# S5 layer of a four-layer decoder trunk: state loads moved into the feed-forward layer, two pairs' states kept as two terms, weight splits tied behind the turned outputs

## The chip, the cores and the metric

The kernel runs on one core of a Trainium2 chip. The core's engines work side by side, each through its own list in order: TensorE (PE) multiplies matrices, VectorE (DVE) and ScalarE (ACT) work elementwise, GpSimd (POOL) does small things, and SyncE (SP) issues the DMA transfers. The metric is the time of one execution in microseconds (us), lower is better.

## The reference

Four layers of 1024 channels on 256 positions, each a mixer, a normed residual, a dense SwiGLU feed-forward layer, and a second normed residual; the mixers are HGRN2, mLSTM, S5, HGRN2. All is fp32. The change is in the S5 mixer: 64 groups of 16 channels, each with 64 complex states that decay by a diagonal factor.

```python
u = x @ w_in
dt = exp(log_dt)[:, None];  abar = exp((a_re + 1j * a_im) * dt)
bbar = (abar - 1) / a * b
h[t] = abar * h[t-1] + bbar @ u[t]          # per group, causal
y[t] = re(c @ h[t]) + d_skip * u[t]
za, zb = split(gelu(y) @ w_out)
out = za * sigmoid(zb)
```

## The kernel before

A weight of 1024 x 256 words (1 MB) is loaded by `fetch` on SP's queue into one of three staging buffers; `stage_next` later makes two pairs from it, a high part on ACT (`hi`, L149) and the low rest on DVE (`lo`, L150). A product is three matmuls, high by high, high by low, low by high (L180 to L182). Since the three buffers go round, a load can start only when the low split of the weight three places ahead is done. A scheduler sets the order on each engine; the code adds edges where it wants another. `self.behind` holds one instruction, and `order` puts each low split behind it.

The S5 mixer (`s5`) works with time in 4 chunks of 64 positions. `project` gives u; `land` turns it on DVE into `s5u` (L1161). The 64 groups go in four pairs p = 0 to 3 of two blocks (e). For a pair:

- `load_in` brings two matrices `bm` (512 KB each) and the table of rotations `cs` (768 KB); `load_out` brings `ch` (512 KB) and two `cw` (256 KB each).
- `inputs` (PE, L1184, 128 small matmuls) gives the states' inputs `g`; a pair's `s5u` must be there.
- `forth` (DVE): four products L1195 and L1196 rotate the inputs, L1197 adds, four scans L1200 run along time with decay `rr`.
- `back` (DVE): products L1206 and L1207 rotate back into the scratch tiles `s5rot`, and the add L1209 writes the states `s5hs`, one of two buffers by turns.
- `outputs` (PE): 32 matmuls of `s5u` with `cw` (L1223) and 64 of the states with `ch` (L1230) into two banks of tag `t`, then gelu on ACT into `ys`.
- `turn`: four transposes of `ys` on PE (L1240), the high cast on ACT (L93, `xx`) and the low rest on DVE (L1245, `xx`). The turn frees the bank it read, and its result is what the next output matmuls read.

Between them `few` issues some of the output product's matmuls (`a`, weights `w_so`) to fill PE. The order in the code is: turn 0 in the middle of the last piece of u, turn 1 before pair 3's inputs, turn 2 before pair 3's outputs, turn 3 last. Each `back` sets `self.behind`.

Of the kernel before, what the change touches and what calls it, by code (L numbers as in the profile page):

```python
# [2 lines left out]

# [6 lines left out]
F32 = mybir.dt.float32  # L10
# [4 lines left out]
ALU = mybir.AluOpType  # L15
AX = mybir.AxisListType

P = 128
# [10 lines left out]
MASKED = (1, 2, 4, 8, 16)  # L29
BIG = 1e30  # L30
AHEAD = 1
ROWS = (0, 1, NBLK - 1)


class Trunk:
    def __init__(self, ctx, tc, aps):
        self.ctx, self.tc, self.nc, self.a = ctx, tc, tc.nc, aps
        mk = lambda name, bufs, **kw: ctx.enter_context(tc.tile_pool(name=name, bufs=bufs, **kw))
        self.const = mk("const", 1)
        self.stage = mk("stage", 3)  # L40
        self.split = mk("split", 8)
        self.xp = mk("xp", 3)
        self.gbp = mk("gbp", 1)
        self.small = mk("small", 4)
        self.ps = mk("ps", 2, space=bass.MemoryType.PSUM)
        self.dram = mk("dram", 1, space=bass.MemoryType.DRAM)
        self.n = 0
        c = self.const
        self.ident = c.tile([P, P], F32, name="ident")
        self.root = c.tile([P, 8], F32, name="root")  # L50
        self.nc.gpsimd.memset(self.root, -0.5)
        self.eps = c.tile([P, 1], F32, name="eps")
        self.nc.gpsimd.memset(self.eps, LN_EPS)
        self.xx = c.tile([P, KD, 2, S], F32R, name="xx")
        self.xh, self.xl = (self.xx[:, :, i] for i in range(2))
        self.x = [None, None]
        self.lb = None
        self.tabled, self.loaded, self.table_name = [], None, None
        self.plan, self.ready, self.staged, self.taken = [], {}, 0, 0
        self.fetched, self.landed = 0, {}  # L60
        self.behind = None

    def uid(self, s):
        self.n += 1
# [73 lines left out]

    def order(self, i, j):

        if j is not None:
            dep = mybir.DependencyInfo(mybir.DependencyClass.NoSync, mybir.DependencyReason.DATA)
            self.tc.add_manual_dep(i, j.name, dep, reason="order")

# [745 lines left out]
    def s5_prepare(self):  # L890


        nc, a = self.nc, self.a
# [4 lines left out]
        c = self.s5const  # L898
# [18 lines left out]
        def temps(*shape):  # L917
            n = int(np.prod(shape))
            dims = "abcd"[: len(shape)]
            out = []  # L920
            for tag, bufs in (("t0", 1), ("t1", 1)):
                t = tile_(tag, [P, 1024], bufs=bufs)[:, :n]
                kw = dict(zip(dims, shape))
                out.append(t.rearrange(f"p ({' '.join(dims)}) -> p {' '.join(dims)}", **kw))
            return out
# [84 lines left out]

        def table_out(b):
            cs, neg = k["cs"], temps(16, 64)[0]
            nc.scalar.mul(neg, cs[:, 1], -1.0)
            for i in range(2):
                for row, x in enumerate((cs[:, 0], neg, cs[:, 1])):
                    nc.sync.dma_start(self.s5_cs[2 * b + i][:, :, row].rearrange("p e (f c) -> p e f c", f=4),
                                      x[:, 8 * i : 8 * i + 8].rearrange("p (e f) c -> p e f c", e=2))
# [92 lines left out]
    def s5(self, gb):  # L1110
# [14 lines left out]
            for i in range(2):  # L1125
                out_piece(n, h, k0, i)

        with tc.tile_pool(name=self.uid("s5"), bufs=1, reuse_waits="tile") as mp, \
                tc.tile_pool(name=self.uid("sw"), bufs=2, reuse_waits="tile") as wp:
            tl = lambda tag, shape, bufs=2: wp.tile(shape, F32, tag=tag, name=self.uid(tag), bufs=bufs)  # L1130
            u = mp.tile([P, 32, 64], F32, name="s5u")
            rr = [mp.tile([P, 2, 4, 64], F32, name=f"s5rr{i}") for i in range(2)]
            hs = [mp.tile([P, 2, 2, 4, 65], F32, name=f"s5hs{i}") for i in range(2)]
            rot = [mp.tile([P, 2, 2, 256], F32, name=f"s5rot{i}") for i in range(3)]
            for r in rr:
                nc.gpsimd.memset(r[:, :, :, 0:1], 0.0)
            for h in hs:
                nc.gpsimd.memset(h[:, :, :, :, 0:1], 0.0)
            bm, cw, ch, tables, wi, pxs = {}, {}, {}, {}, {}, {}

            def load(dst, tag, src, i, bufs=2):
# [10 lines left out]
                for b in (2 * p, 2 * p + 1):  # L1152
                    load(cw, "cw", self.s5_cw, b, 4)

            load_in(0)
            load_out(0)

            def land(ps, f0, h):

# [41 lines left out]

            def back(p):

                x, g, y = rot
                h, cs = hs[p % 2], tables[p]
                tt(x, g, cs[:, :, 0:1].broadcast_to([P, 2, 2, 256]), ALU.mult)  # L1206
                tt(y, g[:, :, ::-1], cs[:, :, 2:0:-1], ALU.mult)  # L1207
                many = lambda t: t.rearrange("p e r (f c) -> p (e r f) c", f=4)
                return tt(h.rearrange("p e r f c -> p (e r f) c")[:, :, 1:], many(x), many(y), ALU.add).ins  # L1209

            pieces, todo = [], []
            col = lambda f: slice(f * P, (f + 1) * P)
# [1 line left out]
            def outputs(p):  # L1214


                py, h = [self.bank("t") for _ in range(2)], hs[p % 2]
                at = lambda g, e, f: py[g][64 * e : 64 * e + 64, 64 * f : 64 * f + 64].rearrange("p (j c) -> p j c", j=4)
                for f in range(4):
                    for g in range(2):  # L1220
                        for e in range(2):
                            w = cw[2 * p + e].rearrange("p (f j g c) -> p f j g c", f=4, j=4, g=2)
                            nc.tensor.matmul(at(g, e, f), u[:, 8 * p + 4 * e + f, :], w[:, f, :, g, :], start=f == 0, stop=False, skip_group_check=True)  # L1223
                for f in range(4):
                    for i in range(2):
                        for g in range(2):
                            for e in range(2):
                                r = slice(64 * g, 64 * g + 64)
                                c = ch[p].rearrange("p i j (f c) -> p i j f c", f=8)
                                nc.tensor.matmul(at(g, e, f), h[r, e, i, f, 0:64], c[r, i, :, 4 * e + f, :], start=False, stop=f == 3 and i == 1, skip_group_check=True)  # L1230
                ys = tl("ys", [P, 4, P], 1)
                for g in range(2):
                    self.act(ys.rearrange("p j (f g c) -> p g f j c", f=4, g=2)[:, g], py[g][:, 0:256].rearrange("p (f j c) -> p f j c", f=4, j=4), AF.Gelu_apprx_tanh)
                todo.append((ys, 2 * p))

            def turn(ys, k):

                pt = self.bank("t")
                for j in range(4):
                    nc.tensor.transpose(pt[:, col(j)], ys[:, j], self.ident)  # L1240
                k = slice(k, k + 2)
                oh, ol = (x[:, k].rearrange("p e (c j) -> p j e c", j=4) for x in (self.xh, self.xl))
                src = pt.rearrange("p (j e c) -> p j e c", j=4, e=2)
                self.act(oh, src, AF.Copy)
                tt(ol, src, oh.bitcast(F32), ALU.subtract)  # L1245
                pieces.extend((h, k.start, i) for i in range(2) for h in range(2))

            def few(n):
# [4 lines left out]
            land(project_part(1, 0, "g"), 0, 1)  # L1253
            self.table("gelu_apprx_tanh_and_others")
            inputs(0)
            load_in(1)
            self.fetch()
            last = project_part(1, 1, "a")
            forth(0)
            land(last, 8, 1)  # L1260
            more = project(1, 0, "a")
            self.behind = back(0)
            load_out(1)
            self.fetch()
            inputs(1)
            load_in(2)
# [4 lines left out]
            land(more, 16, 0)  # L1271
            more = project(1, 1, "a", lambda: turn(*todo.pop(0)))
            land(more, 16, 1)
            self.behind = back(1)
            load_out(2)
            inputs(2)
            load_in(3)
# [4 lines left out]
            few(3)  # L1282
            turn(*todo.pop(0))
            few(1)
            self.behind = back(2)
            load_out(3)
            inputs(3)
            outputs(2)
# [4 lines left out]
            few(3)  # L1293
            turn(*todo.pop(0))
            few(1)
            self.behind = back(3)
            few(2)
            outputs(3)
            self.stage_next()
            few(2)  # L1300
            self.stage_next()

            self.behind = None
            first = banks[0]
            banks[0] = [self.bank("g") for _ in range(2)]
            out_part(1, 0, 0)
# [1 line left out]
            out_part(1, 0, 2)  # L1308
            second, banks[0] = banks[0], first
            turn(*todo.pop(0))  # L1310
        with tc.tile_pool(name=self.uid("so"), bufs=2, reuse_waits="tile") as op:
            self.table("sigmoid_and_others")
            outs = [[], []]

            def gated(h):
                pa, pb = banks[h]
                sg = op.tile([P, 512], F32, tag="sg", name=self.uid("sg"))
                ho = op.tile([P, 512], F32, tag="ho", name=self.uid("ho"), bufs=4)
                self.act(sg, pb, AF.Sigmoid)
                tt(ho, sg, pa, ALU.mult)  # L1320
                outs[h].append(ho)

            gb = gb()
            for h in range(2):
                out_part(0, h, 6)
                gated(h)
            banks = [second, [self.bank("a") for _ in range(2)]]
            for h in range(2):
                for k in (4, 6) if h == 0 else range(0, KD, 2):
                    out_part(1, h, k)  # L1330
                gated(h)
                self.layernorm(h, outs[h], gb)
# [158 lines left out]
```

## Time and profile before

| what | value |
|---|---|
| median of 3 runs | 1262.62 us (1261.2 to 1262.99) |
| the profiled execution | 1260.97 us, span 1259.2 us, mean granted clock 0.997 |
| PE, DVE, ACT busy | 1240.1, 957.9, 705.8 us |
| share of the chain that ended last | PE 94%, DVE 3% |
| the S5 layer's four pairs | about 653 to 717 us of the span |

The span is the stretch from the first to the last instruction of one profiled execution. Busy shares are averages over stages; the chain is followed back from the last instruction, at each step to what released it. A wait is named by the waiting line and by what ended last of what it waited for. The granted clock is 1.0 at full speed of PE.

### The profile page before, as it was taken

The numbers are of one execution on the slowest core, as the hardware profiler recorded it, in microseconds if no ns is written. First come the engines' busy times: TensorE is split into PE (matmuls) and PEld (weight loads), VectorE is DVE, ScalarE is ACT, GpSimd is POOL, SyncE is SP. The second block draws the span as 40 slices with busy tenths as digits, with TensorE's granted clock in tenths as the row PEclk, the third lists the DMA queues.
The fourth block names the chain that finished last, engine by engine and source line by source line (L and its number), as shares of the span: only waits on it lengthen the run. The fifth ranks groups of instructions, "written<-read, shape, count | busy, mean of one in ns | idle before, by whom it ended". The sixth has DMA issues, their size and how long they took to land.

```text
span 1259.2 us, 21464 instructions
## 1 busy us (share of the span) xinstructions
PE 1240.1 (98%) x8525; PEld 1037.3 (82%) x8525; DVE 957.9 (76%) x1704; ACT 705.8 (56%) x1146; POOL 35.9 (3%) x58
## 2 busy tenths in 40 slices
PE   9999999999999999999997999999999999999997
PEld 7977788888788888888886788888889878888886
DVE  6887899876787799866599787666586887766664
ACT  7755576565467555666443456555459654555551
POOL 0000000000100100000000000000000000000000
PEclk9999999999999999999999999999999999999999
DMA  8733466765273276656577446454545432755530
GB/s 324 287 136 134 170 220 230 251 229 200 101 294 134 101 259 233 236 202 231 177 301 290 181 171 247 184 201 181 187 158 220 166 135 99 269 178 190 192 142 34
DMA packets 46340, 247.91 MB, mean 197 GB/s; under 512 B 5504, under 2 KB 11024, under 8 KB 19872
## 3 DMA queue, kind: packets, MB, share of 16 engines
q1 hardware_dynamic: 46112, 246.46, 53.8%
q8 instruction: 67, 1.10, 0.3%
q14 instruction: 33, 0.27, 0.1%
q0 software_dynamic: 128, 0.09, 0.0%
HBM read 233.94 MB, written 12.58 MB: 196 GB/s over the span
## 4 chain that ended last, share of the span: by engine, by line
PE 94%; DVE 3%; DMA 1%; ACT 1%; issue 0%; SPq 0%; DVEq 0%; ACTq 0%
PE g L210 19%; PE g L180 10%; PE g L182 10%; PE g L181 10%; PE g L213 10%; PE a L181 9%; PE a L180 9%; PE a L182 9%; PE a L369 1%; PE t L271 1%; PE a L663 1%; PE t L1074 1%; PE a L543 1%; DVE s5rot L1200 1%; DMA w<-in_w_hg 1%; DMA first<-in_first 1%
## 5 line engine op out<-in xcount | busy, mean ns | idle before, releaser
L150 DVE TENSOR_TENSOR lo<-w,hi 128x1024 fp32r<-128x1024 f32 x388 | 470.7, 1220 | 117.2 <-ACT hi L149 109.7
L149 ACT CAST hi<-w 128x1024 fp32r<-128x1024 f32 x388 | 405.5, 1051 | 195.8 <-PE a L181 109.9
L210 PE MATMUL g<-xx,hi 128*128 128x512 f32 x1024 | 358.2, 395 | 0.0
L213 PE MATMUL g<-xx,lo 128*128 128x256 f32 x1024 | 267.1, 281 | 0.0
L210 PEld LDWEIGHTS g<-xx,hi 128*128 128x128 f32 x1024 | 186.7, 188 | 34.6
L213 PEld LDWEIGHTS g<-xx,lo 128*128 128x128 f32 x1024 | 192.5, 188 | 10.3
L180 PE MATMUL g<-hi,xx 128*128 128x512 f32 (+1 forms) x416 | 167.2, 403 | 2.3 <-ACT xx L290 1.8
L182 PE MATMUL g<-lo,xx 128*128 128x512 f32 (+1 forms) x416 | 165.1, 399 | 0.1
L181 PE MATMUL g<-hi,xx 128*128 128x512 f32 (+1 forms) x416 | 164.7, 397 | 0.0
L350 ACT COPY sum<-g 128x256 f32<-128x256 f32 x128 | 47.7, 373 | 147.8 <-PE g L210 147.6
L180 PE MATMUL a<-hi,hh 128*128 128x512 f32 x328 | 129.4, 395 | 0.0
L182 PE MATMUL a<-lo,hh 128*128 128x512 f32 x328 | 129.3, 394 | 0.0
L181 PE MATMUL a<-hi,hl 128*128 128x512 f32 x328 | 128.8, 393 | 0.0
L351 DVE TENSOR_TENSOR sum<-g,sum 128x256 f32<-128x256 f32 x128 | 54.1, 423 | 69.4 <-ACT sum L350 68.8
L180 PEld LDWEIGHTS g<-hi,xx 128*128 128x128 f32 x416 | 78.3, 188 | 20.1 <-ACT xx L290 2.7
L182 PEld LDWEIGHTS g<-lo,xx 128*128 128x128 f32 x416 | 78.2, 188 | 18.2 <-DVE lo L150 1.4
L181 PEld LDWEIGHTS g<-hi,xx 128*128 128x128 f32 x416 | 78.3, 188 | 15.9
L182 PEld LDWEIGHTS a<-lo,hh 128*128 128x128 f32 x328 | 61.5, 188 | 14.5
L181 PEld LDWEIGHTS a<-hi,hl 128*128 128x128 f32 x328 | 61.5, 188 | 14.3 <-DVE hl L340 0.2
L180 PEld LDWEIGHTS a<-hi,hh 128*128 128x128 f32 x328 | 61.5, 188 | 12.5 <-ACT hh L339 0.2
L180 PE MATMUL g<-xx,hi 128*128 128x256 f32 x192 | 54.5, 284 | 0.2 <-DVE k L614 0.2
L182 PE MATMUL g<-xx,hi 128*128 128x256 f32 x192 | 54.3, 283 | 0.0
(305 smaller groups left out, 1754.9 us busy)
## 6 DMA issues: line engine op xcount, KB each, us to landing
w<-in_w_gu SPq DMA_DIRECT2D x88, 1024.0 KB, 4.9
w<-in_w_dn SPq DMA_DIRECT2D x44, 1024.0 KB, 4.8
w<-in_w_hg SPq DMA_DIRECT2D x30, 1024.0 KB, 5.2
w<-in_w_ml SPq DMA_DIRECT2D x12, 1024.0 KB, 4.9
gb<-in_ln SPq DMA_DIRECT2D x8, 1024.0 KB, 4.8
w<-in_w_ho SPq DMA_DIRECT2D x8, 1024.0 KB, 4.8
w<-in_w_so SPq DMA_DIRECT2D x8, 1024.0 KB, 6.7
s5b<-st SPq DMA_DIRECT2D x16, 256.0 KB, 2.0
```

Source lines behind the costliest of these rows:

```text
L149: self.nc.scalar.copy(hi, x)
L150: i = self.nc.vector.tensor_tensor(lo, x, hi.bitcast(F32), ALU.subtract).ins
L180: mm(ps, lh, rh, start=start, stop=False)
L181: mm(ps, ll, rh, start=False, stop=False)
L182: mm(ps, lh, rl, start=False, stop=stop)
L210: whole = lambda: mm(ps, hi[:, c], self.xx[:, k].rearrange("p i t -> p (i t)"), start=k == 0, stop=k == KD - 1)
L213: mm(ps[:, S:], lo[:, c], self.xh[:, k], start=False, stop=False)
L271: nc.tensor.transpose(pt[:, (k % 4) * P : (k % 4 + 1) * P], z[:, k * P : (k + 1) * P], self.ident)
L350: nc.scalar.copy(t, ps[:, S:])
L351: nc.vector.tensor_tensor(t, ps[:, 0:S], t, ALU.add)
L369: nc.tensor.matmul(down[h][n], hidden(h, j, b)[x], dn[j][b][y][:, f], start=False, stop=(x, y, b) == steps[-1])
L543: nc.tensor.matmul(o, att[:, 2 * h + hd % 2, :], v[:, h, c], start=True, stop=h == 0)
```

## The change

- The loads of all `bm` and `cs` of pairs 0 and 1 (four times 512 KB, twice 768 KB) are asked for at the layer's start. The state buffers now lie in three pools (`sh`, `sm`, `sw`), and those of `bm` and `cs` are free early enough that on SP's queue the six loads stand in feed-forward layer 1, between its weights; `ch` and `cw` of these pairs stay behind the first output weight. The second output weight and the parameters `gb` now stand ahead of pair 2's `bm`, the third ahead of pair 3's first `bm` and pair 2's `cs`.
- The states `s5hs` are flat tiles of 1025 words; column 63 of each table is set to zero on GpSimd when the tables are built, so that a run of 64 words starts with a zero or with the state before.
- For pairs 1 and 2 (`TWO`) the back products write `s5hs0` and `s5hs1` themselves, there is no add, and `outputs` runs 128 state matmuls, both terms summed in the bank.
- `self.behind` holds two instructions, the end of the last `back` and the last turn's low rest, and each low split is put behind both.

Lines move by two at the start and by up to ten at the end (L1184 is L1190, L1195/L1196 L1201/L1202, L1197 L1203, L1200 L1206, L1206/L1207 L1216/L1217, L1209 L1219, L1223 L1234, L1230 L1240, L1240 L1250, L1245 L1255, L149/L150 L151/L152, L93 L95).

```diff
+TWO = (1, 2)
...
-        self.behind = None
+        self.behind = {}
...
-        if j is not None:
+        for j in j.values():
...
             cs, neg = k["cs"], temps(16, 64)[0]
+            nc.gpsimd.memset(cs[:, :, :, 63:64], 0.0)
...
+            hp, mp, wp = (pools.enter_context(tc.tile_pool(name=self.uid(n), bufs=1, reuse_waits="tile")) for n in ("sh", "sm", "sw"))
+            tl = lambda tag, shape, bufs=2: (wp if tag in ("bm", "cs") else hp).tile(shape, F32, tag=tag, name=self.uid(tag), bufs=bufs)
...
-            hs = [mp.tile([P, 2, 2, 4, 65], F32, name=f"s5hs{i}") for i in range(2)]
+            hs = [hp.tile([P, 1025], F32, name=f"s5hs{i}") for i in range(2)]
...
-            load_in(0)
-            load_out(0)
+            for p in range(2):
+                load_in(p)
+                load_out(p)
...
             def back(p):
...
-                h, cs = hs[p % 2], tables[p]
+                cs, flat = tables[p], lambda t: t.rearrange("p e r x -> p (e r x)")
+                at = lambda h: h[:, 1:].rearrange("p (e r x) -> p e r x", e=2, r=2)
+                x, y = map(at, hs) if p in TWO else (x, y)
                 tt(x, g, cs[:, :, 0:1].broadcast_to([P, 2, 2, 256]), ALU.mult)
-                tt(y, g[:, :, ::-1], cs[:, :, 2:0:-1], ALU.mult)
...
+                i = tt(y, g[:, :, ::-1], cs[:, :, 2:0:-1], ALU.mult)
+                if p not in TWO:
+                    i = tt(hs[p % 2][:, 1:], flat(x), flat(y), ALU.add)
+                self.behind["back"] = i.ins
...
+                py, terms = [self.bank("t") for _ in range(2)], hs if p in TWO else hs[p % 2 :][:1]
...
+                for f, i, h in itertools.product(range(4), range(2), terms):
+                    for g, e in itertools.product(range(2), range(2)):
+                        r, x = slice(64 * g, 64 * g + 64), 64 * (8 * e + 4 * i + f)
+                        last = f == 3 and i == 1 and h is terms[-1]
+                        nc.tensor.matmul(at(g, e, f), h[r, x : x + 64], c[r, i, :, 4 * e + f, :], start=False, stop=last, skip_group_check=True)
...
-                tt(ol, src, oh.bitcast(F32), ALU.subtract)
+                self.behind["turn"] = tt(ol, src, oh.bitcast(F32), ALU.subtract).ins
...
-            self.behind = None
...
             turn(*todo.pop(0))
+            self.behind = {}
```

What it does to the order shows at three places. The first is ACT, from the gelu of pair 1's outputs to turn 2's cast. `hi` are the high casts of the output weights; `xx` are the turns' casts. Before:

```order
L93 ACTIVATE ys1295_7462<-t1293_7412 128x4x4x16 [waits PE_49,Activation_49]
L93 ACTIVATE ys1295_7462<-t1294_7413 128x4x4x16 [waits PE_49]
L149 CAST hi1316_7662<-w1300_7483 128x1024
L93 ACTIVATE xx_83<-t1305_7507 128x4x2x64 [waits PE_49]
L149 CAST hi1324_7769<-w1318_7666 128x1024 [waits DMAHW4_49]
L149 CAST hi1326_7773<-w1318_7666 128x1024
L93 ACTIVATE ys1313_7645<-t1311_7595 128x4x4x16 [waits PE_49,Activation_49]
L93 ACTIVATE ys1313_7645<-t1312_7596 128x4x4x16 [waits PE_49]
L149 CAST hi1328_7789<-w1319_7668 128x1024 [waits DMAHW5_49]
L149 CAST hi1330_7793<-w1319_7668 128x1024
L93 ACTIVATE xx_83<-t1320_7688 128x4x2x64 [waits PE_49]
```

And after:

```order
L95 ACTIVATE ys1296_7498<-t1294_7416 128x4x4x16 [waits PE_49,Activation_49]
L95 ACTIVATE ys1296_7498<-t1295_7417 128x4x4x16 [waits PE_49]
L151 CAST hi1329_7856<-w1320_7735 128x1024 [waits DMAHW5_49,PE_49]
L95 ACTIVATE xx_83<-t1306_7543 128x4x2x64 [waits PE_49]
L151 CAST hi1331_7860<-w1320_7735 128x1024 [waits PE_49]
L95 ACTIVATE ys1314_7712<-t1312_7630 128x4x4x16 [waits PE_49,Activation_49]
L95 ACTIVATE ys1314_7712<-t1313_7631 128x4x4x16 [waits PE_49]
L151 CAST hi1336_7880<-w1335_7878 128x1024 [waits DMAHW7_49,DVE_49,PE_49]
L95 ACTIVATE xx_83<-t1321_7755 128x4x2x64 [waits PE_49]
```

The first high cast of the fifth output weight (`w1320`, which was `w1319`) moves ahead of turn 1's cast, and that of the sixth (`w1335`, which was `w1334`) ahead of turn 2's. The second place is DVE, from pair 2's scans to pair 3's first products. Before:

```order
L1200 SCALAR_TENSOR_TENSOR s5rot1_6907<-s5rr0_6902,s5rot0_6906 128x256 x3
L1245 TENSOR_TENSOR xx_83<-t1305_7507,xx_83 128x4x2x64 [waits Activation_49]
L1206 TENSOR_TENSOR s5rot0_6906<-s5rot1_6907,cs1274_7222 128x1024 [waits DVE_49]
L1207 TENSOR_TENSOR s5rot2_6908<-s5rot1_6907,cs1274_7222 128x1024
L1209 TENSOR_TENSOR s5hs0_6904<-s5rot0_6906,s5rot2_6908 128x16x64 [waits DVE_49]
L150 TENSOR_TENSOR lo1315_7659<-w1300_7483,hi1314_7658 128x1024 [waits DMAHW7_49]
```

And after:

```order
L1206 SCALAR_TENSOR_TENSOR s5rot1_6912<-s5rr0_6907,s5rot0_6911 128x256 x3
L1216 TENSOR_TENSOR s5hs0_6909<-s5rot1_6912,cs1275_7227 128x1024 [waits DVE_49,PE_49]
L1217 TENSOR_TENSOR s5hs1_6910<-s5rot1_6912,cs1275_7227 128x1024 [waits PE_49]
L1255 TENSOR_TENSOR xx_83<-t1306_7543,xx_83 128x4x2x64 [waits Activation_49]
L152 TENSOR_TENSOR lo1316_7726<-w1301_7519,hi1315_7725 128x1024 [waits DMAHW2_49]
```

The add is gone, and turn 1's low rest moves from ahead of the back products to behind them. Turns 0 and 2 move likewise: turn 0's from ahead of pair 1's scans to behind them, turn 2's from between pair 3's back products to behind its state add. The third place is PE, from turn 2's transposes on. `a` is the output product, `t` the outputs of pair 3. Before, the first of the 32 matmuls with `cw` stand ahead of the wait for turn 2's low rest:

```order
L180 MATMUL a1301_7485<-hi1314_7658,xx_83 128x512 [waits Activation_49]
L180 MATMUL a1303_7487<-hi1314_7658,xx_83 128x512
L1223 MATMUL t1321_7716<-cw1307_7525,s5u_6901 64x64 [waits DMAHW2_49,PE_49]
L1223 MATMUL t1321_7716<-cw1308_7527,s5u_6901 64x64 [waits DMAHW3_49]
...
L181 MATMUL a1301_7485<-hi1314_7658,xx_83 128x512 [waits DVE_49]
L182 MATMUL a1301_7485<-lo1315_7659,xx_83 128x512
```

After, all 32 stand behind the output product's matmuls:

```order
L182 MATMUL a1302_7521<-hi1315_7725,xx_83 128x512 [waits Activation_49]
L183 MATMUL a1302_7521<-hi1315_7725,xx_83 128x512 [waits DVE_49]
L184 MATMUL a1302_7521<-lo1316_7726,xx_83 128x512
...
L184 MATMUL a1304_7523<-lo1316_7726,xx_83 128x512
L1234 MATMUL t1322_7783<-cw1308_7560,s5u_6906 64x64 [waits DMAHW2_49,PE_49]
L1234 MATMUL t1322_7783<-cw1309_7562,s5u_6906 64x64 [waits DMAHW3_49]
```

PE waits for the low rest right behind the first matmul of that group, with 11 of them, the 32 and pair 3's state matmuls still to come. In pair 2's outputs likewise: from the third matmul of L1234 on, all of them and the 128 state matmuls stand behind turn 1's low rest, whose bank they use.

More of the change, by code (lines that the diff above doesn't have):

```diff
@@ L1 @@
+import itertools
 import math
@@ L1126, in out_part @@
                 out_piece(n, h, k0, i)
-        with tc.tile_pool(name=self.uid("s5"), bufs=1, reuse_waits="tile") as mp, \
-                tc.tile_pool(name=self.uid("sw"), bufs=2, reuse_waits="tile") as wp:
-            tl = lambda tag, shape, bufs=2: wp.tile(shape, F32, tag=tag, name=self.uid(tag), bufs=bufs)
+        with ExitStack() as pools:
+            hp, mp, wp = (pools.enter_context(tc.tile_pool(name=self.uid(n), bufs=1, reuse_waits="tile")) for n in ("sh", "sm", "sw"))
+            tl = lambda tag, shape, bufs=2: (wp if tag in ("bm", "cs") else hp).tile(shape, F32, tag=tag, name=self.uid(tag), bufs=bufs)
             u = mp.tile([P, 32, 64], F32, name="s5u")
-            rr = [mp.tile([P, 2, 4, 64], F32, name=f"s5rr{i}") for i in range(2)]
-            hs = [mp.tile([P, 2, 2, 4, 65], F32, name=f"s5hs{i}") for i in range(2)]
+            rr = [hp.tile([P, 2, 4, 64], F32, name=f"s5rr{i}") for i in range(2)]
+            hs = [hp.tile([P, 1025], F32, name=f"s5hs{i}") for i in range(2)]
             rot = [mp.tile([P, 2, 2, 256], F32, name=f"s5rot{i}") for i in range(3)]
@@ L1137, in s5 @@
             for h in hs:
-                nc.gpsimd.memset(h[:, :, :, :, 0:1], 0.0)
+                nc.gpsimd.memset(h[:, 0:1], 0.0)
             bm, cw, ch, tables, wi, pxs = {}, {}, {}, {}, {}, {}
@@ L1204, in back @@
                 x, g, y = rot
-                h, cs = hs[p % 2], tables[p]
+                cs, flat = tables[p], lambda t: t.rearrange("p e r x -> p (e r x)")
+                at = lambda h: h[:, 1:].rearrange("p (e r x) -> p e r x", e=2, r=2)
+                x, y = map(at, hs) if p in TWO else (x, y)
                 tt(x, g, cs[:, :, 0:1].broadcast_to([P, 2, 2, 256]), ALU.mult)
-                tt(y, g[:, :, ::-1], cs[:, :, 2:0:-1], ALU.mult)
-                many = lambda t: t.rearrange("p e r (f c) -> p (e r f) c", f=4)
-                return tt(h.rearrange("p e r f c -> p (e r f) c")[:, :, 1:], many(x), many(y), ALU.add).ins
+                i = tt(y, g[:, :, ::-1], cs[:, :, 2:0:-1], ALU.mult)
+                if p not in TWO:
+                    i = tt(hs[p % 2][:, 1:], flat(x), flat(y), ALU.add)
+                self.behind["back"] = i.ins
             pieces, todo = [], []
@@ L1214, in outputs @@
             def outputs(p):
-                py, h = [self.bank("t") for _ in range(2)], hs[p % 2]
+                py, terms = [self.bank("t") for _ in range(2)], hs if p in TWO else hs[p % 2 :][:1]
                 at = lambda g, e, f: py[g][64 * e : 64 * e + 64, 64 * f : 64 * f + 64].rearrange("p (j c) -> p j c", j=4)
@@ L1223, in outputs @@
                             nc.tensor.matmul(at(g, e, f), u[:, 8 * p + 4 * e + f, :], w[:, f, :, g, :], start=f == 0, stop=False, skip_group_check=True)
[L1224 to L1230, printed above, removed]
+                c = ch[p].rearrange("p i j (f c) -> p i j f c", f=8)
+                for f, i, h in itertools.product(range(4), range(2), terms):
[3 more added lines that the diff above has]
+                        nc.tensor.matmul(at(g, e, f), h[r, x : x + 64], c[r, i, :, 4 * e + f, :], start=False, stop=last, skip_group_check=True)
                 ys = tl("ys", [P, 4, P], 1)
@@ L1261, in s5 @@
             more = project(1, 0, "a")
-            self.behind = back(0)
-            load_out(1)
+            back(0)
             self.fetch()
@@ L1273, in s5 @@
             land(more, 16, 1)
-            self.behind = back(1)
+            back(1)
             load_out(2)
@@ L1284, in s5 @@
             few(1)
-            self.behind = back(2)
+            back(2)
             load_out(3)
@@ L1295, in s5 @@
             few(1)
-            self.behind = back(3)
+            back(3)
             few(2)
```

1 line of the change is left out of this document (removed).

## Prediction

> **What bounds the kernel now.** I read the page's busy table and its chain first, then the busy time by stage, then what TensorE waits for, and last the timelines of the S5 layer.
>
> ```profile
> PE 1240.1 (98%) x8525; PEld 1037.3 (82%) x8525; DVE 957.9 (76%) x1704; ACT 705.8 (56%) x1146; POOL 35.9 (3%) x58
> PE 94%; DVE 3%; DMA 1%; ACT 1%; issue 0%; SPq 0%; DVEq 0%; ACTq 0%
> ```
>
> TensorE (PE) is busy 98% of 1259.2 us and carries 94% of the chain that ends last; VectorE (DVE) carries 3%. The change can only gain where the chain leaves PE. That is one stretch, the four pairs of the S5 layer. In the table by stage (stretch, its length, busy time of PE, PEld, DVE, ACT, POOL, granted clock, DMA share, GB/s):
>
> ```profile
> 480.00:490.00 10.00, 10.00 (x56) 8.60 (x56) 9.92 (x20) 5.84 (x12) 0.00 (x0) 1.00 0.51 200
> 644.00:648.00 4.00, 3.54 (x19) 2.73 (x18) 3.85 (x11) 0.37 (x1) 0.72 (x1) 1.00 1.03 424
> 671.00:680.00 9.00, 6.99 (x185) 5.52 (x187) 8.50 (x11) 2.30 (x3) 0.00 (x0) 1.00 0.86 302
> 680.00:693.00 13.00, 10.21 (x276) 8.44 (x278) 12.93 (x16) 5.11 (x7) 0.00 (x0) 1.00 0.93 360
> 690.60:694.00 3.40, 1.43 (x66) 1.32 (x66) 3.37 (x4) 2.00 (x3) 0.00 (x0) 1.00 0.86 354
> 694.00:697.40 3.40, 3.40 (x10) 2.63 (x9) 3.40 (x6) 2.36 (x4) 0.00 (x0) 0.51 0.04 14
> ```
>
> From 671 to 693 us DVE is full and PE is idle for 2.0 + 2.8 us. After the idle stretch at 690.6 the granted clock is 0.51 for 3.4 us. PE's waits in the whole layer:
>
> ```profile
> PE t L1230 <- DVE s5hs L1209: 2.5, 1, 2.5
> PE g L1184 <- issue: 1.9, 1, 1.9
> PE g L1184 <- DVE s5u L1161: 1.6, 1, 1.6
> PE a L181 <- DVE xx L1245: 0.5, 1, 0.5
> ```
>
> The state add L1209 and the low half of a turn, L1245, are what PE waits for. The second wait has no releaser; in the chain it comes at the end of a burst of small matmuls, and DVE works through it, so it costs nothing later. The chain (start, us, what) there and at the end of pair 3:
>
> ```profile
> 661.00 1.92 PE g L1184 x126
> 662.92 1.87 issue
> 665.09 1.08 PE t L1223 x32
> 703.13 0.50 PE a L181
> 705.73 0.61 PE t L1223 x16
> 706.34 1.09 PE t L1230 x64
> ```
>
> At 703.13 PE is released by the turn's L1245, and at 707.43 (706.34 + 1.09) pair 3's outputs are done; from there PE has enough work, so what 707.43 becomes is what the time gains or loses. DVE's timeline (start, us, line; idle in brackets) gives the steps that lead there:
>
> ```profile
> 670.45 1.22 DVE L1197 TENSOR_TENSOR s5rot<-s5rot,s5rot 128x1024 f32<-128x1024 f32 x1
> 672.10 1.07 DVE L1245 TENSOR_TENSOR xx<-t,xx 128x512 fp32r<-128x512 f32 x1 [0.43 <-ACT xx L93]
> 673.08 2.43 DVE L1200 TENSOR_TENSOR_SCAN s5rot<-s5rr,s5rot 128x256 f32<-128x256 f32 x4
> 675.54 1.23 DVE L1206 TENSOR_TENSOR s5rot<-s5rot,cs 128x1024 f32<-128x1024 f32 x1
> 676.68 0.71 DVE L1161 STREAM_TRANSPOSE s5u<-a 128x512 f32<-128x512 f32 x1
> 677.32 1.18 DVE L1207 TENSOR_TENSOR s5rot<-s5rot,cs 128x1024 f32<-128x1024 f32 x1
> 678.53 1.23 DVE L1209 TENSOR_TENSOR s5hs<-s5rot,s5rot 128x1024 f32<-128x1024 f32 x1
> 679.67 1.22 DVE L150 TENSOR_TENSOR lo<-w,hi 128x1024 fp32r<-128x1024 f32 x1
> 680.81 0.68 DVE L1195 TENSOR_TENSOR s5rot<-g,cs 128x512 f32<-128x512 f32 x1
> 683.21 1.22 DVE L150 TENSOR_TENSOR lo<-w,hi 128x1024 fp32r<-128x1024 f32 x1
> 684.34 1.22 DVE L1197 TENSOR_TENSOR s5rot<-s5rot,s5rot 128x1024 f32<-128x1024 f32 x1
> 685.59 2.44 DVE L1200 TENSOR_TENSOR_SCAN s5rot<-s5rr,s5rot 128x256 f32<-128x256 f32 x4
> 692.43 1.22 DVE L150 TENSOR_TENSOR lo<-w,hi 128x1024 fp32r<-128x1024 f32 x1
> 695.96 1.21 DVE L150 TENSOR_TENSOR lo<-w,hi 128x1024 fp32r<-128x1024 f32 x1
> 701.96 1.11 DVE L1245 TENSOR_TENSOR xx<-t,xx 128x512 fp32r<-128x512 f32 x1
> 704.22 1.23 DVE L1209 TENSOR_TENSOR s5hs<-s5rot,s5rot 128x1024 f32<-128x1024 f32 x1
> ```
>
> From start to start a 128x1024 operation takes 1.14 us (1.25 where the next needs its result), the scan 2.46, s5u 0.64, the back product L1207 1.21, four products 2.40 (680.81 to 683.21), a turn's low half 0.98. ScalarE (ACT) and the queue on SyncE (SP) give the price of a weight:
>
> ```profile
> 447.97 2.00 ACT L149 CAST hi<-w 128x1024 fp32r<-128x1024 f32 x2 [2.98 <-DMA w<-in_w_gu]
> 679.37 1.05 ACT L149 CAST hi<-w 128x1024 fp32r<-128x1024 f32 x1 [3.22 <-DMA w<-in_w_so]
> 684.94 1.10 ACT L93 ACTIVATE xx<-t 128x512 fp32r<-128x512 f32 x1 [2.24 <-PE t L1240]
> 697.24 0.33 SPq L108 DMA_DIRECT2D w<-in_w_so  x1
> 701.99 2.00 ACT L149 CAST hi<-w 128x1024 fp32r<-128x1024 f32 x2 [0.75 <-DMA w<-in_w_so]
> ```
>
> The load at 697.24 goes out as the low split at 695.96 ends (697.17), because the two share a buffer, and its cast starts at 701.99: 4.75 us from issue to cast.
>
> **The change, part by part.**
>
> *Loads in the feed-forward layer.* Of the S5 loads four bm and two cs (3.5 MB), leave the stretch at 640 us. What it is worth there: at 644 to 648 the DMA share is 1.03, but PE's only idle there, 0.46 us, is not put to a load; I take 0, with 0.46 as the gain's bound. In feed-forward layer 1 they add 3.5 MB at some 420 GB/s (the rate of that saturated row), 8.3 us of transfer, where a stage such as 480 to 490 has a DMA share of 0.51 and PE fully busy. Of the casts between 440 and 540 us one waits for a load, the 2.98 us at 447.97, and PE does not stop for it. The worst place is a bm pair, 1 MB, right ahead of a weight: 2.4 us later. I take 0, bounds 0 and +2.4. The two memsets on GpSimd (POOL busy 3%) and the flat states cost nothing: the operations keep their sizes.
>
> *Two terms.* Pairs 1 and 2 lose L1209, 1.14 us of DVE each, and PE gets 64 more state matmuls for each, 1.09 us by the row at 706.34. Both lie where PE has idle time, so they cost PE nothing while it waits for DVE.
>
> *The ties.* DVE, walked in its new order from the end of L1197 at 671.67 (up to there its order is as before): scan to 674.15; the turn's low half, now behind the scan, to 675.15 (its 0.43 us of waiting is gone); back product to 676.3, s5u to 676.9, back product to 678.1; no add; low split to 679.25 where before it ended at 680.81; products to 681.65, low split to 682.8. So far 1.54 us are won: 1.14 for the add, 0.40 for the wait. Then add 684.05, scan 686.5, back products 687.65 and 688.85.
>
> Next comes turn 1's low half, and this is where I see the gain go. On ACT the high cast of the fifth output weight now stands ahead of turn 1's own cast (the first order list of the section on the change). That weight's load goes out when the low split frees its buffer, at 682.8; its cast starts 4.75 us later, 687.55, ends 688.6; the turn's cast ends 689.7, and the low half on DVE 690.7. PE waits for it before pair 2's outputs. In its timeline before, the inputs of pair 3 were
>
> ```profile
> 686.23 1.99 PE L1184 MATMUL g<-s5u,bm 128*32 128x64 f32 x128
> ```
>
> and ended at 688.2. Now they end about there too: s5u is ready 0.4 us sooner (676.9 for 677.3), pair 1's state matmuls last 1.1 us longer, and their wait for L1209 is gone (0.4, with hs0 written first). So PE idles from 688.3 to 690.7, 2.4 us; behind the wait are 30 of L1234 and the 128 state matmuls. Before, DVE began the next low split at 692.43; now at 690.7, 1.7 us ahead instead of 2.5.
>
> From 690.7: low split 691.85, products 694.25, low split 695.4, add 696.65, scan 699.1, back products 700.25 and 701.45, state add 702.6. Behind it, no longer between the back products, stands turn 2's low half. Its cast again has a weight's cast ahead of it: load out at 695.45, cast 700.2 to 701.25, turn's cast to 702.35. So DVE is the later one: 702.6 to 703.65, where L1245 before ended at 703.07 (701.96 + 1.11). What DVE won, 2.8 us at the state add (before 705.45), is spent by standing 2.3 us further back.
>
> PE then has 11 matmuls (703.13 to 705.73, 2.60), all 32 of L1234 (1.08; before 16 were done ahead) and the 64 state matmuls (1.09): 703.7 + 4.77 = 708.5, against 707.43. **+1.05 us**.
>
> *What hides in the waits.* The burst on PE is now 128 + 120 matmuls in pair 1 and 30 + 128 in pair 2. The row at 662.92 shows a stop of 1.87 us in such a burst. In pair 1 it would delay turn 1's transposes, whose cast began at 684.94 before and cannot begin before 688.6 now, 3.7 us of room; in pair 2 PE ends its outputs at 693.95, plus 24 matmuls of 0.236 us (2.60 / 11) and four transposes some 700, plus 1.87 still ahead of 702.35. So 0, bounds 0 and +1.9.
> [...]
>
> *Clock.* By the rows at 690.6 and 694.0, 1.43 us of work in 3.4 us was followed by 3.4 us at 0.51. Before, that loss of some 1.7 us lay in PE's spare time ahead of 703. Now the first wait (2.4 us) can bring it on again and it is absorbed as before, since PE is early at the second wait. If it is not brought on there, PE reaches the second wait at 700 and idles for up to 3.4 us but for one matmul, and the half clock falls on the closing 4.77 us: up to +1.7. I take 0 and keep +1.7.
> [...]
>
> The sum against the profiled execution (1260.97 us; span 1259.2): 1262.0. That execution is 1.65 us under the median of the runs, 1262.62; put on the median: 1263.7.
>
> **The rivals.** *The half clock falls on the end* (+1.7 more, +2.7): 1265.4. For it: a gap of the same length did it once, and the second wait now stands straight ahead of pair 3's outputs. Against: the first wait is likely to use it up. It decides if PE works less than about 1.4 of the 3.4 us ahead of 703.7.
> *The saved DVE time arrives, faster.* If turn casts on ACT are not held by the weights, turn 1's low half starts at 688.85 and all that follows moves up by 0.85: only +0.2. For a real gain PE must get to pair 3's outputs without the turn: then the state add at 702.6, 2.8 us earlier than before, would set the end, 1262.62 - 2.8 = 1259.8. The outer bound is all waits, 6.5, less the added 2.2 us of matmuls: -4.3, 1258.3. Against: PE's order puts the 11 matmuls that read turn 2's low half ahead of pair 3's outputs.
> *Weights late in feed-forward layer 1*, +2.4 alone, +3.4 with the sum: 1266.1. Against: full PE and a DMA share of 0.5 to 0.8 there. It decides if a moved load stands ahead of a weight whose cast has under 2.4 us to spare.
> *The change does nothing that lasts*: 1262.6, from the same balance with both terms 0.5 us smaller.
>
> **How the numbers follow.** About 0.2% (2.5 us) is what a measurement of this kernel can tell from no change: under 1260.1 is faster, above 1265.1 slower. The forecast with its near kin (0 to +2): 0.58. Half clock at the end 0.2, late weights 0.07: of their 0.27 nearly all is slower. The saved time arrives: 0.15, nearly all faster. Range 1259.8 (the state add sets the end) to 1266.2 (either of the slower two).
>
> **What would show it.** In the changed profile: PE waits for L1255 of turn 1 near 688 to 691 in place of L1209's 2.5 us; ACT's cast of w_so with a DMA wait right ahead of the turn's cast, twice; DVE reaches pair 3's state add near 701.5, then L1255; pair 3's state matmuls end near 708.5; no new PE wait between 440 and 640. Wrong if L1255 of turn 2 ends before 702 (faster) or the granted clock between 703 and 709 is near 0.75 (slower).

## The result: 0.35% slower, and where the time went

| | before | after |
|---|---|---|
| median | 1262.17 us | 1266.06 us |
| runs | 1260.98 to 1262.99 | 1265.38 to 1268.86 |
| profiled execution, span | 1260.97, 1259.2 us | 1265.98, 1264.2 us |

The ratio is 1.0035, with a 95% interval of 1.0024 to 1.0045: 3.9 us slower by the medians, 5.0 by the profiled executions. The forecast was no measurable change, 1263.7.

The page of the changed kernel, busy table and chain:

```profile
PE 1245.4 (99%) x8653; PEld 1041.9 (82%) x8653; DVE 955.3 (76%) x1702; ACT 706.1 (56%) x1146; POOL 36.5 (3%) x60
PE 95%; DVE 2%; ACT 1%; issue 1%; DMA 1%; SPq 0%; DVEq 0%; ACTq 0%
```

DVE lost two records and 2.6 us, PE gained 128, and "issue", time in which an engine waits for nothing the profile shows, has come into the chain with 1%. By stage, as before (length, busy time of PE, PEld, DVE, ACT, POOL, clock, DMA share, GB/s):

```profile
440.00:500.00 60.00, 60.00 (x297) 49.67 (x296) 57.28 (x119) 33.44 (x52) 1.53 (x5) 1.00 0.81 297
671.00:680.00 9.00, 9.00 (x193) 7.06 (x191) 8.93 (x12) 5.43 (x6) 0.00 (x0) 1.00 0.79 279
680.00:693.00 13.00, 10.09 (x147) 8.38 (x145) 8.74 (x11) 2.61 (x4) 0.00 (x0) 0.74 0.49 181
693.00:703.00 10.00, 9.45 (x306) 8.05 (x306) 9.71 (x13) 1.90 (x4) 0.00 (x0) 1.00 0.28 98
```

The moved loads raise the DMA share of feed-forward layer 1, from 0.65 between 440 and 500 us in the kernel before to 0.81, and PE stays full there (60.00 of 60 us in both). From 671 to 680 us PE's idle time is gone. The loss begins between 680 and 693: PE idles 2.9 us, the granted clock is 0.74, and DVE, full before, is busy for 8.74 of 13 us. What PE waits for:

```profile
PE t L1240 <- issue: 3.5, 2, 2.9
PE g L1190 <- issue: 2.2, 1, 2.2
PE a L183 <- DVE xx L1255: 0.8, 1, 0.8
PE a L182 <- ACT xx L95: 0.6, 1, 0.6
```

The 2.5 us for the state add and the 1.6 us for s5u are gone, as the change has it. In their place stands a stop of 2.9 us in pair 1's state matmuls (L1240) with no releaser. The chain shows what hangs on it:

```profile
680.09 1.43 PE t L1240 x84
681.52 2.91 issue
684.43 1.33 PE t L1240 x27
...
691.62 0.45 PE t L1250 x4
692.09 1.10 ACT xx L95
...
706.30 1.08 DVE xx L1255
707.42 0.50 PE a L183
...
710.25 1.08 PE t L1234 x32
711.33 1.09 PE t L1240 x64
```

After 84 of the last 120 state matmuls PE stands still until 684.43. The 36 that are left (the chain shows 27 of them) take 1.33 us where 84 had taken 1.43, and the long matmuls behind them start 0.43 us apart until 690.3, not 0.23. It is half clock for 6.8 us, by the row

```profile
683.70:690.50 6.80, 6.07 (x47) 4.94 (x47) 5.04 (x7) 1.65 (x3) 0.00 (x0) 0.50 0.64 236
```

So the last of turn 1's transposes end at 692.1, and DVE waits for turn 1's cast. DVE's timeline:

```profile
678.07 1.21 DVE L152 TENSOR_TENSOR lo<-w,hi 128x1024 fp32r<-128x1024 f32 x1
687.66 1.22 DVE L1217 TENSOR_TENSOR s5hs<-s5rot,cs 128x1024 f32<-128x1024 f32 x1
693.22 1.19 DVE L1255 TENSOR_TENSOR xx<-t,xx 128x512 fp32r<-128x512 f32 x1 [4.34 <-ACT xx L95]
705.16 1.23 DVE L1219 TENSOR_TENSOR s5hs<-s5rot,s5rot 128x1024 f32<-128x1024 f32 x1
706.30 1.06 DVE L1255 TENSOR_TENSOR xx<-t,xx 128x512 fp32r<-128x512 f32 x1
```

and ACT's:

```profile
689.51 1.04 ACT L151 CAST hi<-w 128x1024 fp32r<-128x1024 f32 x1 [3.15 <-PE a L183]
692.09 1.09 ACT L95 ACTIVATE xx<-t 128x512 fp32r<-128x512 f32 x1 [1.54 <-PE t L1250]
704.02 1.05 ACT L151 CAST hi<-w 128x1024 fp32r<-128x1024 f32 x1 [3.93 <-DMA w<-in_w_so]
```

Pair 3's outputs end at 712.42 (711.33 + 1.09) where they ended at 707.43: 5.0 us, which is the whole difference of the spans.

### The profile page after: what moved, and what is told of

Read it like the earlier page. It is cut to its first block, busy times and chain, and to the rows that moved or that the text cites. A ratio compares the mean times of both kernels' runs of the same rounds, so it can differ in the third digit from the quotient of the medians.

```text
span 1264.2 us, 21732 instructions
## 1 busy us (share of the span) xinstructions
PE 1245.4 (99%) x8653; PEld 1041.9 (82%) x8653; DVE 955.3 (76%) x1702; ACT 706.1 (56%) x1146; POOL 36.5 (3%) x60
## 3 DMA queue, kind: packets, MB, share of 16 engines
q8 instruction: 68, 1.11, 0.3%
## 4 chain that ended last, share of the span: by engine, by line
PE 95%; DVE 2%; ACT 1%; issue 1%; DMA 1%; SPq 0%; DVEq 0%; ACTq 0%
PE g L212 19%; PE g L182 10%; PE g L184 10%; PE g L183 10%; PE g L215 10%; PE a L182 9%; PE a L183 9%; PE a L184 9%; PE a L371 1%; PE t L273 1%; PE a L665 1%; PE t L1077 1%; PE a L545 1%; DMA first<-in_first 1%; PE g L1190 0%
## 5 line engine op out<-in xcount | busy, mean ns | idle before, releaser
L152 DVE TENSOR_TENSOR lo<-w,hi 128x1024 fp32r<-128x1024 f32 x388 | 470.4, 1220 | 117.3 <-ACT hi L151 109.9
L151 ACT CAST hi<-w 128x1024 fp32r<-128x1024 f32 x388 | 405.6, 1051 | 197.1 <-PE a L183 115.0
L183 PE MATMUL g<-hi,xx 128*128 128x512 f32 (+1 forms) x416 | 164.8, 397 | 0.0
L183 PE MATMUL a<-hi,hl 128*128 128x512 f32 x328 | 128.8, 393 | 0.0
L183 PEld LDWEIGHTS g<-hi,xx 128*128 128x128 f32 x416 | 78.3, 188 | 15.9
L183 PEld LDWEIGHTS a<-hi,hl 128*128 128x128 f32 x328 | 61.5, 188 | 14.3 <-DVE hl L342 0.2
```

The lines of the kernel that those rows point to most:

```text
L151: self.nc.scalar.copy(hi, x)
L152: i = self.nc.vector.tensor_tensor(lo, x, hi.bitcast(F32), ALU.subtract).ins
L183: mm(ps, ll, rh, start=False, stop=False)
```

## The experiments

Theory A: the stop is PE running out of instructions. The page of the changed kernel shows a queue of instructions:

```profile
q8 instruction: 68, 1.11, 0.3%
```

That is 68 packets of 16 KB (1.11 MB / 68) beside 2 x 8653 PE records (a weight load and a matmul each), one for about 255 records, that is 127 matmuls; the page of before has 67 beside 2 x 8525, about 255 again. By this count they are blocks of PE's instructions. At 84 in 1.43 us, 127 state matmuls last about 2.2 us. Counted in the trace, the stops in the S5 layer come after matmul record 4411 before, and after 4411, 4792 and 5047 in the changed kernel: 3 x 127 and 2 x 127.5 apart. After the edge at record 4665 was passed, at 679.2, an instruction packet started at 682.15 and ended at 683.1, and PE went on at 684.43: 5.2 us after the edge, when the 127 records behind it were through in 2.3. Rivals: B, the moved loads; C, the tie behind the turns; D, the places of the turns' low halves and casts alone, as in the prediction, only dearer.

**No pair in two terms.**

```diff
-TWO = (1, 2)
+TWO = ()
```

> The changed kernel with no pair in two terms: adds back, 64 state matmuls for each pair; the moved loads and the tie stay. Theory A (the burst of 128 input and 120 state matmuls runs PE out of instructions for 2.9 us, the half clock follows, and turn 1's cast comes 2.4 us late): the stop in pair 1's outputs is gone, no wait put to 'issue' there above 0.5 us, turn 1's cast near 685; turns 1 and 2 stand where they stood before the change, so 1261 to 1263. Theory B (the moved loads cost it): 1265 to 1267. Theory C (the tie costs it): 1265 to 1267, DVE idle ahead of a turn.

Measured: 1262.03 us, ratio to the kernel before 1.0 (0.9991 to 1.0009). PE's waits, and ACT's turn 1:

```profile
PE t L1240 <- DVE s5hs L1219: 2.5, 1, 2.5
684.75 1.10 ACT L95 ACTIVATE xx<-t 128x512 fp32r<-128x512 f32 x1 [2.92 <-PE t L1250]
```

The stop in pair 1's outputs is gone, and the old wait for the state add is back. Moved loads and tie cost nothing without the two terms: B and C fall as causes by themselves.

**No tie behind the turn.**

```diff
-                self.behind["turn"] = tt(ol, src, oh.bitcast(F32), ALU.subtract).ins
+                tt(ol, src, oh.bitcast(F32), ALU.subtract)
```

> The changed kernel with the low splits tied behind the back products alone, as before the change, two terms and moved loads kept. In the order turn 1's low half then stands behind both low splits, further back still. Theory A: the stop of about 2.9 us stays, and the time is no better: 1265.5 to 1269. Theory C (the tie costs it): 1262 to 1263.5. Theory B: 1266.

Measured: 1266.93 us, 1.0042 (1.0029 to 1.0056). No better than the changed kernel. A stop of 1.74 us, for the 2.9 expected, stands again after record 4792, and PE waits 3.9 us for turn 2's low half, which has gone behind three low splits. Taking the tie away does not win the time back. But the chain of this run goes past the stop, on DVE, and the half clock does not follow it: the granted clock is 0.97 from 680 to 693 and 0.81 from 703 to 712.

**The loads back in their old place.**

```diff
-            for p in range(2):
-                load_in(p)
-                load_out(p)
+            load_in(0)
+            load_out(0)
...
             inputs(0)
+            load_in(1)
...
             back(0)
+            load_out(1)
```

> The changed kernel with pair 0's loads asked for at the layer's start and pair 1's bm, cs, ch and cw where they were before; two terms, tie and pools kept; the order on DVE stays. Theory A: the stop stays, 2 to 4 us depending on how busy the DMA engines are when the block is fetched: 1265 to 1268. Theory B (the moved loads cost it): 1262 to 1263.

Measured: 1266.89 us, 1.0041 (1.0029 to 1.0054), with stops of 3.18 us after record 4411 and 2.97 after 4792. The time is as theory A had it, and the chain runs through both stops. That a stop's length depends on how busy the DMA engines are is not shown: their share was 0.02 in the stop of 1.87 us in the kernel before, 0.76 in the changed kernel's of 2.23 and 0.36 in its 2.91.

**Long matmuls between the bursts.**

```diff
             inputs(2)
+            few(3)
...
-            few(3)
             turn(*todo.pop(0))
```

> The changed kernel with three pieces of the output product (9 to 18 long matmuls of 0.23 us) between pair 2's inputs and pair 1's outputs instead of behind them, so that the small matmuls do not follow each other without a break; DVE's and ACT's orders stay. Theory A: the stop in pair 1's outputs falls from 2.9 to at most 1.2 us, no half clock after it, turn 1's cast not later than 690, and 1263 to 1264.5. If the place of the low halves and casts alone costs the time (theory D, that of the prediction, too small by 3 us): 1265.5 to 1267.

Measured: 1264.14 us, 1.0023 (1.0013 to 1.0034). PE's, ACT's and DVE's timelines:

```profile
684.06 1.02 PE L1240 MATMUL t<-ch,s5hs 64*64 64x64 f32 x50 [0.35 <-issue]
690.54 1.09 PE L1190 MATMUL g<-s5u,bm 128*32 128x64 f32 x61 [2.23 <-issue]
687.29 1.06 ACT L151 CAST hi<-w 128x1024 fp32r<-128x1024 f32 x1 [1.51 <-DMA w<-in_w_so]
688.25 1.06 ACT L95 ACTIVATE xx<-t 128x512 fp32r<-128x512 f32 x1
689.34 1.10 DVE L1255 TENSOR_TENSOR xx<-t,xx 128x512 fp32r<-128x512 f32 x1 [0.85 <-ACT xx L95]
```

With the nine long matmuls behind the inputs the stop after record 4793 is 0.35 us, and turn 1's low half starts at 689.34. A new stop of 2.23 us stands after record 4920, one edge of 127 further, in pair 3's inputs. By the medians about half of the loss is gone, as A forecast, though the interval overlaps that of the changed kernel. The profiled execution does not show the gain. At 1266.75 us it is one of the two longest of the eight, and pair 3's outputs end at 711.5:

```profile
695.16 6.54 DMA w<-in_w_so
702.76 1.07 ACT xx L95
703.00:712.00 9.00, 7.51 (x110) 5.87 (x111) 7.89 (x7) 2.03 (x4) 0.00 (x0) 0.81 0.41 145
```

The first two lines are of its chain, the third is of the stages. Up to turn 1 it is as A has it. Then turn 2's cast on ACT stands behind a weight's, whose load takes 6.5 us where the prediction had 4.75 from issue to cast, and the clock falls to 0.81: the casts of D, dearer, and the prediction's rival of the half clock at the end.

**Pair 1 alone, pair 2 alone.**

```diff
-TWO = (1, 2)
+TWO = (1,)
```

> The changed kernel with pair 1 alone in two terms. Theory A (the burst of pair 2's inputs and pair 1's 120 state matmuls runs PE out of instructions): the stop stays at the same place, 2 to 3 us, and the time stays at 1265 to 1267.5. If it takes both pairs to lose the time: near the middle, 1264.

Measured: 1266.57 us, 1.003 (1.0018 to 1.0043). PE's timeline, again after record 4792:

```profile
684.15 0.80 PE L1240 MATMUL t<-ch,s5hs 64*64 64x64 f32 x36 [1.86 <-issue]
```

Pair 1 alone loses as much as both. But the trace shows only half of theory A, the stop, a little under the 2 to 3 us expected. The chain and the stages:

```profile
684.08 6.23 DMA w<-in_w_so
690.38 1.05 ACT hi L151
691.43 1.04 ACT xx L95
...
705.41 1.09 DVE xx L1255
706.55 0.60 PE a L183
680.00:693.00 13.00, 10.82 (x341) 9.03 (x329) 11.68 (x15) 4.48 (x7) 0.00 (x0) 1.00 0.58 197
703.00:712.00 9.00, 6.54 (x69) 4.87 (x73) 8.97 (x9) 2.91 (x3) 0.00 (x0) 0.81 0.22 72
```

No half clock follows the stop (1.00), and the chain does not run through it. Turn 1's cast waits for the weight's cast ahead of it and that one for its load, 6.2 us, while the transposes had begun at 688.5. From there the chain goes through DVE to turn 2 behind the state add, and the clock is half at the end. Here theory D holds, and not A. For pair 2 the edit is `TWO = (2,)`.

> The changed kernel with pair 2 alone in two terms. Here turn 1's low half and cast stand where they were before the change, turn 2's low half stands behind pair 3's state add. Theory A: pair 1's outputs have 64 state matmuls again, no stop there; pair 2's 128 follow PE's wait for the states, where instructions have had time to arrive, stop at most 0.5 us; one add less on DVE (1.14) against turn 2 two places further back (2.3): 1262 to 1263.5. If it takes both pairs: 1264.

Measured: 1264.18 us, 1.0011 (1.0002 to 1.002): more than A expected, and the 1264 of the rival that it takes both pairs, which the run with pair 1 alone does not fit. No stop in pair 1's outputs; PE's waits and the stage behind pair 3 say what was left out:

```profile
PE a L183 <- DVE xx L1255: 4.4, 1, 4.4
703.00:712.00 9.00, 8.13 (x111) 6.34 (x112) 7.62 (x7) 1.20 (x4) 0.00 (x0) 0.66 0.53 198
```

PE waits 4.4 us for turn 2's low half behind the state add, and runs the closing stretch at a clock of 0.66. The walk had the place, not the clock.

**The edges moved by 64 records.**

```diff
+                                for _ in range(2 if b == 0 and 16 * i + 4 * f + r // 32 < 40 else 1):
                                     nc.tensor.matmul(px[r : r + 32, ...], bm[b][...], u[...], start=True, stop=True)
```

> The changed kernel with the 32 matmuls of pair 0's first input block issued twice (the same values written again), 64 more records on PE ahead of the place in question, some 0.5 us of work. In the changed kernel the stop came after 4792 matmul records from the start, 84 records into the last 120 of pair 1's state matmuls. Theory A (the stop stands at the edge of a block of instructions): again after 4792 +-2 records, which is now 20 +-2 into these 120; likewise the stop in pair 1's inputs stays at record 4411, 62 into the 128 and no longer 126. If the stop belongs to the place in the program (a bank, a buffer, a wait the profile hides): after 84 and after 126 again.

One run, 1271.45 us, so the time is not compared. PE's timeline:

```profile
659.88 1.50 PE L1191 MATMUL g<-s5u,bm 128*32 128x64 f32 x44 [3.56 <-issue]
689.88 2.66 PE L1241 MATMUL t<-ch,s5hs 64*64 64x64 f32 x100 [3.56 <-issue]
```

The second stop comes after record 4792 again, which is now 20 and not 84 into the 120: it belongs to the count of instructions, not to a bank or a buffer. The first was expected after 4411 and stands one block earlier, after 4284, an edge that the longer burst of pair 0's inputs now reaches.

The traces of all thirteen kernels agree. PE stops 22 times for over 1 us with no releaser, always after record 4284, 4411, 4792 or 4920. In the kernel before and the changed one it goes on at 664.79, 665.19 and 684.43, 1.26, 1.26 and 1.35 us after a packet of the instruction queue has ended (663.53, 663.93 and 683.08). Whether such a stop sets the time is another question. After record 4792 the chain runs through those of 2.9 us and more (the changed kernel, the loads back, this run, and the one below with the turns first), and not through those of 1.74 and 1.86 us.

**The casts' order.** The filled kernel, with each weight's high cast behind the last turn's cast.

```diff
-        self.nc.scalar.copy(hi, x)
+        c = self.nc.scalar.copy(hi, x).ins
+        if "cast" in self.behind:
+            self.order(c, {"cast": self.behind["cast"]})
...
-                self.act(oh, src, AF.Copy)
+                self.behind["cast"] = self.act(oh, src, AF.Copy)
```

> As the run with the filled burst, and each weight's high cast ordered behind the last turn's cast on ACT, so that turns 1 and 2 are not held by a weight's load. Theory A and the prediction's second step together: against the filled run's 1264.1 the walk gives 0.8 us back (turn 1's low half follows pair 2's back products at once): 1262.5 to 1263.8, the waits for L1255 (here L1257) under 1 us in all. If the casts' order is worth nothing: 1264.

Measured: 1264.45 us, 1.001 (1.0001 to 1.0019), where the filled kernel had 1.0023 (1.0013 to 1.0034) against the kernel before of its own series. The intervals overlap, and runs spread from 1261.1 to 1265.7: a gain of 0.8 us can't be told here. The waits for L1257 did not fall below 1 us: PE waits 2.2 us for turn 2's low half, which stands behind the state add on DVE until 704.08, 1.6 us after its cast has ended. Inconclusive on the casts.

**The turns' low halves ahead of the back products.** Each `back` puts its first product behind the last turn's low half:

```diff
-                tt(x, g, cs[:, :, 0:1].broadcast_to([P, 2, 2, 256]), ALU.mult)
+                i = tt(x, g, cs[:, :, 0:1].broadcast_to([P, 2, 2, 256]), ALU.mult).ins
+                self.order(i, {k: v for k, v in self.behind.items() if k == "turn"})
```

with `TWO = (2,)`:

> Pair 2 alone in two terms, as in the earlier run (1264.2), and besides each pair's first back product ordered behind the last turn's low half. In the order turn 2's low half then stands between pair 3's back products, where it stood before the change, not behind the state add. Theory A's second half (turn 2's low half two places further back, 2.3 us, and the half clock after PE's 4.4 us wait for it, cost what the dropped add saves): the wait for turn 2 falls from 4.4 to about 2 us, pair 3's outputs end near 706.3 instead of 711.2, and 1260.5 to 1262.5. If the place of turn 2 is not what costs: 1264.

Measured: 1261.56 us, 0.999 (0.9981 to 0.9999). PE's wait, DVE's turn 2 and the closing stretch:

```profile
PE a L183 <- DVE xx L1256: 1.9, 1, 1.9
699.98 1.05 DVE L1256 TENSOR_TENSOR xx<-t,xx 128x512 fp32r<-128x512 f32 x1
703.00:712.00 9.00, 9.00 (x122) 7.28 (x121) 7.32 (x8) 2.13 (x5) 0.00 (x0) 0.89 0.55 213
```

Turn 2's low half starts 2.7 us sooner than with pair 2 alone (702.73), the wait falls to 1.9 us, the clock stays at 0.89. Pair 3's outputs end at 707.6, later than the 706.3 expected, for what remains of the slow clock. It is the fastest of all, 4.5 us under the changed kernel by the medians and 0.1% under the kernel before, at the edge of what the interval tells from no change. The same with both pairs and no filling:

> The changed kernel (pairs 1 and 2 in two terms, tie and moved loads) with each pair's first back product ordered behind the last turn's low half, nothing against the stop in pair 1's burst. Theory A: the stop of 2 to 3 us after record 4792 stays and turn 1's cast is late as before (689 to 693), only turn 2's place is won back: 1263.5 to 1266. If the places of the low halves were the whole loss: 1262 or less.

Measured: 1269.74 us, 1.0059 (1.0041 to 1.0076), a miss to the slow side. DVE's timeline:

```profile
693.19 1.20 DVE L1256 TENSOR_TENSOR xx<-t,xx 128x512 fp32r<-128x512 f32 x1 [5.47 <-ACT xx L95]
708.20 1.12 DVE L1256 TENSOR_TENSOR xx<-t,xx 128x512 fp32r<-128x512 f32 x1 [3.32 <-ACT xx L95]
```

The stop after record 4792 (2.91 us) still makes turn 1's cast late, and now pair 2's back product stands behind it too: the tie turns the stop into more DVE idle time. Turn 2's place is not won back, and the granted clock is 0.75 from 703 to 712. With the filling and the casts' order:

> Pairs 1 and 2 in two terms with the filled burst, the weights' casts behind the turns' casts, and each pair's first back product behind the last turn's low half: everything named so far mended. Walk: the filled run's 1264.3, less up to 2.3 for turn 2's place: 1262 to 1263.5; what stays is the stop of 1.5 to 2.2 us after record 4920, in pair 3's inputs. Without any effect of the places: 1264.

Measured: 1263.48 us, 1.001 (1.0 to 1.002). PE's largest wait is

```profile
PE g L1192 <- issue: 3.5, 2, 2.0
```

with the stop of 1.96 us after record 4920. The median and the stop are as expected, but that the stop is what stays is not shown: the profiled execution has it in its chain and takes 1260.93 us, the least of the twelve. The five executions of 1264.8 us and more have a mean granted clock of 0.995 or 0.996, the other seven 0.997 to 0.999. So what stays goes largely with the clock, and why it falls in some executions and not in others is open.

## Why the prediction was wrong, point by point

- *Loads in the feed-forward layer*, taken as 0: right. PE has no new wait between 440 and 640 us, and the run without two terms, which keeps loads and tie, stands at the time of before.
- *Two terms, DVE's side*: right to 0.1 us. The walk had the low split after pair 1 at 678.1 and pair 2's last product ending at 688.85; they stand at 678.07 and 687.66 + 1.22.
- *Two terms, PE's side*: "Both lie where PE has idle time, so they cost PE nothing while it waits for DVE", and under *What hides in the waits* the stop, seen as 1.87 us in the trace of before, was taken as "0, bounds 0 and +1.9". **This step failed**: the stop was put at nothing because turn 1's transposes were thought to have 3.7 us of room. In the changed kernel's profile they start at 691.46, before at 684.30, 7.2 us later. The stop is 2.9 of it. The half clock behind it, which the term left out, is some 3.0 (11 long matmuls from 685.76 to 690.69 in 4.9 us for 2.6, and 0.7 in the small ones). The 64 more state matmuls are 1.1, which the room had not counted. Turn 1's low half came at 693.2 for the walk's 689.7. That 3.5 us goes through DVE's chain and is 3.9 at the end, 712.4 for the walk's 708.5. With the walk's own +1.05 it makes the 5.0 us.
- *The clock*: that a gap brings half clock held in the changed kernel's profile (0.50 behind the stop of 2.91 us), its size and place did not. The forecast had 3.4 us of it and a loss of 1.7; it was 6.8 us and some 3.0. The rival put it at the end of pair 3, and the changed kernel's profile has it in the middle (0.50 from 683.7 to 690.5, 1.00 from 703 to 712). At the end it fell with pair 2 alone (0.66), and in the profiles without the tie, with the loads back, with the filling and with pair 1 alone (0.81 from 703 to 712 in each).
- *The cast ahead of turn 1*: not shown by the changed kernel, where that weight's cast itself waited for PE (3.15 us, L183) and was over at 690.55, a microsecond ahead of the transposes. It stands as forecast in the filled kernel: 687.29, 688.25, 689.34 for the walk's 687.55, 688.6, 689.7. Ahead of turn 2 it stands in both (704.02, waiting for the load). In the filled kernel's profile turn 2's low half waits 1.42 us for it; in the changed kernel, where it follows the state add, it costs nothing that the trace shows.
- *Turn 2 behind the state add*: right. L1219 starts at 705.16 and L1255 follows at 706.30. Putting it back with pair 2 alone gave 2.6 us (1264.18 to 1261.56).

PE passes most edges without a stop of over 1 us: of the 66 between the 67 blocks of the kernel before one had such a stop, of the 67 of the changed kernel two. All 22 of the thirteen kernels, 1.5 to 3.6 us long, stand in bursts of small matmuls.

That the measured 1266.06 us lies inside the range is luck: its upper end came from the half clock at the end and from late weights, and the changed kernel's profile shows neither.

Open: the size of a stop (1.74 to 3.56 us after the same record 4792) follows no rule that these runs settle. The account by the stop is shown for the profiles whose chain runs through it, the changed kernel's above all. Without the tie and with pair 1 alone as much was lost on another path, by the turns' places and casts, a load of 6.2 us and the half clock at the end. The half clock was not taken away by itself, and it does not decide the time alone. Of the changed kernel's six executions the one of 1265.38 us has a mean granted clock of 0.998, the profiled one, 1265.98 us, 0.994. So how the 3.9 us between the medians divide between the stop and the places is not separated: filling the burst gave 1.9 us by the medians, with intervals that overlap.

## What to carry to other kernels

Count instructions, not only time: here a run of 248 tiny matmuls passed record 4665 at 679.2 us and reached 4792 at 681.5, and PE went on only at 684.4. An engine that looks idle enough to take more work may have no more instructions to give. Nine long matmuls between two bursts cut the stop from 2.91 to 0.35 us here, and a new one of 2.23 us stood one edge further. When a remedy is judged by its median, look also at what its profiled execution took: here one was among the longest of its kernel and another the shortest. And when a wait goes away, look for the path that was nearly as long: here turn 1 was also held by a weight's load and cast. An operation taken off one engine is worth having only if it does not change what its neighbours are ordered behind: the same two-term idea gained 0.1% with pair 2 alone and the turn kept in its place, and lost 0.59% with both pairs and the turn kept in its place, 0.35% without.

## What the runs showed of the hardware

Where PE stopped after an edge, it went on 4.0 us (without the two terms, after 4411) to 6.5 us (with the filling, 684.06 to 690.54) after the edge before had been passed; this is read from the timelines of the ten kernels up to the one with the casts' order. PE passed 4284 at 660.6 and went on at 664.8 in the kernel before, 4665 at 679.2 and 684.4 in the changed one, 684.1 and 689.9 with the edges moved. The last instruction packet ahead of that took 0.95 us in the kernel before and 0.94 us in the changed one. Not every edge costs that: the kernel before passed 4792 at 686.3 and the next edge at 688.5 without a stop. Why is not shown.

And a gap of 2.9 us, followed by small matmuls, brought half clock for 6.8 us, twice as long as after the 2.5 us gap before. The length of the gap does not settle it: 2.97 us with the loads back brought half the length of that (0.50 from 687.4 to 690.7), and 1.86 us with pair 1 alone none (1.00 from 680 to 693).
